# A two-layer hybrid model step on one core: feed-forward input as seven block products in place of eight, weight-block sums by adding transfers, output projection in six parts

## The chip, the cores and the metric

The kernel runs on one core of a Trainium2 chip. The metric is the device time of one execution in microseconds (us), lower is better. TensorE (PE) multiplies; VectorE (DVE), ScalarE (ACT) and GpSimd (POOL) work on vectors; SyncE (SP) issues most transfers. PSUM is the memory that matmuls write, in banks of 512 float32 for each of 128 partitions.

## What is computed

Two layers over 640 tokens (128 of context, 512 latent) of 1024 features. Each layer is a feed-forward half step, a token mixing and a second feed-forward half step, every one behind an RMS norm that is modulated by shift, scale and gate ("ada" rows, from a condition vector). The change is in the feed-forward:

```python
def swiglu(h, w_in, w_out):
    g, u = jnp.split(h @ w_in, 2, axis=-1)
    return (jax.nn.silu(g) * u) @ w_out

def layer(x, cond, p, lam_init, ropes, ctx):
    mods = (jax.nn.silu(cond) @ p['w_ada'] + p['b_ada']).reshape(cond.shape[0], N_MOD, 1, D_MODEL)
    ...
    h = modulate(rmsnorm(x, p['norm_ffn1']), sh1, sc1)
    x = x + 0.5 * g1 * swiglu(h, p['w_ffn1_in'], p['w_ffn1_out'])
    h = modulate(rmsnorm(x, p['norm_mix']), sh2, sc2)
    y, kv = token_mix(h, p, lam_init, ropes, ctx)
    x = x + g2 * y
    h = modulate(rmsnorm(x, p['norm_ffn2']), sh3, sc3)
    x = x + 0.5 * g3 * swiglu(h, p['w_ffn2_in'], p['w_ffn2_out'])
```

The feed-forward is 2816 wide, so `w_in` has 22 tiles of 128 columns for the gate and 22 for the value.

## The kernel before, in words

The residual stream is kept as 8 tiles `x[d]` of 128 features by 640 tokens. All large products are float32 in three passes: weight and activation are each split into a part `hi` that the multiplier takes exactly and a rest `lo`, and hi·hi, hi·lo and lo·hi are summed in PSUM. `split` (L166 to L168) makes an activation's two parts: ACT copies (L167), DVE subtracts (L168). `load_w` (L143 to L158) loads a weight block through SP into one of three `raw` buffers (L144), ACT makes `hi` (L156), DVE makes `lo` (L157).

The sublayers run in the order feed-forward (0,0), mix of layer 0, feed-forward (0,2), (1,0), mix of layer 1, (1,2), the last one with the final norm. A feed-forward (`ffn`) goes over 22 pairs of a gate tile and a value tile. `pair` takes for each of both a 512 KB weight block, and 8 contraction tiles x 3 passes x 2 halves of the tokens (320 and 322 columns; two columns carry the shift) are 48 matmuls into one PSUM tile `S` of two banks; there are two such tiles. DVE takes the product out of PSUM times the norm's factor `R` (L385), ACT applies silu (L421), DVE multiplies (L423), and `split` makes the pair's activation. After 8, 7 and 7 pairs (`PARTS`) the output projection `out` adds what these pairs give to all 8 tiles of `x` (`x_update`, L366). In the last part each `out` also prepares the next norm's tile (`Norm.tile`: squares on ACT L289, sum on POOL L291, scaled hi and lo L300 and L301).

Beside this runs the "pump": 131 steps that each load 512 KB of the ada weights and reduce them on DVE with two instructions (`dump`, L244). `tick` takes steps at a rate of 0.8, 0.8 and 0.55 in the first three feed-forwards: 2 x rate for a pair and 1 x rate for an `out`.

The order of the instructions on each engine is set when the program is built, by a scheduler of the framework: it takes the program in the order in which it is written, knows which tile each instruction reads and writes, and places semaphore waits between engines by whole tiles. Each engine then runs its own list in that order.

Of the kernel before, what the change touches and what calls it, by code (L numbers as in the profile page):

```python
# [20 lines left out]
NO, NE = 1, 6  # L21
# [15 lines left out]
PARTS = ((0, 8), (8, 15), (15, 22))  # L37
# [4 lines left out]
# the two halves of the tokens, without and with the columns of the shift  # L42
# [4 lines left out]
# columns of the per-partition vector table  # L47
# [28 lines left out]
def hybrid_step(ctx: ExitStack, tc: tile.TileContext, x_in, cc_in, cb_in, w_ada0, w_ada, pv_in, lam_in, w_fin, w_fout, w_min, w_mout,  # L76
# [7 lines left out]
    up = ctx.enter_context(tc.tile_pool(name="up", bufs=35))  # L84
    tp = ctx.enter_context(tc.tile_pool(name="tp", bufs=5))
    sp = ctx.enter_context(tc.tile_pool(name="sp", bufs=32))
# [17 lines left out]
    def E(dt=F32):  # L104
        return tp.tile([128, N], dt, tag="e", name=nm("e"), bufs=5)
# [37 lines left out]
    def load_raw(src, n):  # L143
        raw = wp.tile([128, 1024], F32, tag="raw", name=nm("raw"), bufs=3)  # L144
        nc.sync.dma_start(raw[:, :n], src)
        return raw

    def load_w(src, n, eng=None):
        """DRAM [128, n] -> (hi, lo) with hi + lo the weights exactly."""
        raw = load_raw(src, n)  # L150
        return split_w(raw, n, eng)

    def split_w(raw, n, eng=None):
        hi = wp.tile([128, 1024], F32R, tag="hi", name=nm("hi"), bufs=2)
# [17 lines left out]
    def lambdas():  # L172
        lv = T()
        nc.sync.dma_start(lv[:, :L * 128], lam_in)
        for l in range(L):
# [11 lines left out]
            lam.append(lm)  # holds -(lambda)  # L187
# [11 lines left out]
    def ada_direct(c, loads):  # L199
        """the products; yields before the row is turned into columns."""  # L200
# [20 lines left out]
    def silu_rows():  # L221
        """silu of the two conditions, along the free dimension of every partition."""
# [38 lines left out]
    def gate_tiles(l, sub):  # L261
        if sub == 1:
            return [mods[l][2 * (3 * sub + 2) + h] for h in range(2)]
        r = []
        for h in range(2):
            t = C([128, 4, 2], name="gate")
            V.tensor_scalar(out=t, in0=mods[l][2 * (3 * sub + 2) + h], scalar1=0.5, scalar2=None, op0=ALU.mult)
            r.append(t)
        return r

    class Norm:
        """Prepares the moving operand of the next sub-layer tile by tile."""
# [49 lines left out]
        def stats_spread(self):  # L322
# [4 lines left out]
            R = tp.tile([128, TX], F32, tag="R", name=nm("R"), bufs=1)  # L327
            G.memset(R[:, N:TX], 1.0)
            S.activation(R[:, :512], pa, AF.Copy)
            S.activation(R[:, 512:N], pb[:, :128], AF.Copy)  # L330
            self.R = R

# [10 lines left out]
    def mm3(ps, cuts, hi, lo, acts, ks=range(KT), start=True, stop=True, hs=(0, 1)):  # L343
        """ps[h] (+)= w^T act over contraction tiles, three passes."""
        for i, k in enumerate(ks):
            w0, w1 = hi[:, k * 128:(k + 1) * 128], lo[:, k * 128:(k + 1) * 128]
            ah, al = acts[k]
            for p, (w, a) in enumerate(((w0, ah), (w0, al), (w1, ah))):
                for h in hs:
                    c0, c1 = cuts[h]  # L350
                    mm(ps[h][:, :c1 - c0], w, a[:, c0:c1],
                       start and i == 0 and p == 0, stop and i == len(ks) - 1 and p == 2)

    def halves(p):
        """the two halves of the tokens with the shift, side by side across the banks of p."""
# [5 lines left out]
    def x_update(d, ps, gate):  # L361
        """x[d] += gate * ps, ps holding the two halves of the tokens."""
# [7 lines left out]
    def ffn(l, sub, norm, nxt, pump, prate):  # L370
# [11 lines left out]
        def pair(i):  # L382
            def evac(ps):
                t = T()
                V.tensor_tensor(out=t[:, :TX], in0=whole(ps), in1=norm.R, op=ALU.mult)  # L385
                return t
# [948 lines left out]
```

## Time and profile before

| what | value |
|---|---|
| time, median of 3 executions | 2506.04 us (2505.41 to 2507.21) |
| the profiled execution's span | 2509.4 us |
| PE busy | 2446.1 us, 97% |
| DVE busy | 1563.7 us, 62% |
| ACT busy | 865.5 us, 34% |
| POOL busy | 304.9 us, 12% |
| bytes moved by transfers | 282.10 MB |

Busy time is the union of an engine's instructions over the span of the profiled execution. A mean over the span hides that stages differ, so the rows further down are windows of single stages.

### The profile page before, as it was taken

Reading aid. Unit: us, or ns where it says so; the run is one execution under the profiler, and the core shown is the slowest. Engines: PE = TensorE matmul, PEld = TensorE weight load, DVE = VectorE, ACT = ScalarE, POOL = GpSimd, SP = SyncE. Lnnn points to the kernel's source line nnn. Section 1 sums busy time; section 2 is a strip of 40 time slices with the busy share of each in tenths; the row PEclk is TensorE's granted clock in tenths of the full one; section 3 lists DMA queues with packets and bytes.
Section 4 is the critical chain, followed back from the end, with each engine's and each line's share of the span. In section 5 each row is a group of like instructions: output and inputs, shape, how many; then the busy total and the mean of one; then the engine's idle time right before and its main releaser. Section 6 shows DMA issues by size and latency. Waiting matters only on the chain. (4 is left out here: it accounts for less than half of the span.)

```text
span 2509.4 us, 39961 instructions
## 1 busy us (share of the span) xinstructions
PE 2446.1 (97%) x16529; PEld 2405.3 (96%) x16529; DVE 1563.7 (62%) x2550; ACT 865.5 (34%) x1417; POOL 304.9 (12%) x329
## 2 busy tenths in 40 slices
PE   8999999998998999999999999999999999999998
PEld 4999999998898999999999999999989999999998
DVE  5766766668886666666666556556788664334335
ACT  3222212356664221212332122224666442122223
POOL 3000000143224000000110000003513230000002
PEclk8999999999999999999999999999999999999999
DMA  7444444224322444444333333332242122222224
GB/s 261 154 142 136 132 138 138 90 89 137 117 66 89 137 135 135 133 137 135 101 110 110 120 115 116 115 102 89 90 143 85 53 74 70 75 76 70 82 72 130
DMA packets 91317, 282.10 MB, mean 112 GB/s; under 512 B 9600, under 2 KB 17664, under 8 KB 91136
## 3 DMA queue, kind: packets, MB, share of 16 engines
q1 hardware_dynamic: 91136, 279.56, 34.6%
q8 instruction: 130, 2.13, 0.3%
q14 instruction: 51, 0.42, 0.1%
HBM read 264.58 MB, written 14.94 MB: 111 GB/s over the span
## 5 line engine op out<-in xcount | busy, mean ns | idle before, releaser
L128 PE MATMUL S<-u,hi 128*128 128x320 f32 (+1 forms) x9056 | 1720.7, 311 | 14.8 <-DVE x L366 7.3
L128 PEld LDWEIGHTS S<-u,hi 128*128 128x128 f32 x9056 | 1434.7, 189 | 18.8 <-ACT hi L156 7.7
L128 PE MATMUL S<-u,lo 128*128 128x320 f32 (+2 forms) x4528 | 1047.6, 310 | 4.4 <-DVE lo L157 4.4
L128 PEld LDWEIGHTS S<-u,lo 128*128 128x128 f32 x4528 | 765.2, 189 | 5.4 <-DVE lo L157 5.4
L156 ACT ACTIVATE hi<-raw 128x1024 fp32r<-128x1024 f32 (+2 forms) x336 | 345.2, 1027 | 1117.7 <-PE S L128 649.9
L244 DVE SCALAR_TENSOR_TENSOR dump<-raw,sc 128x1024 f32<-128x1024 f32 x262 | 322.9, 1234 | 175.9 <-DMA raw<-in_w_ada_dram 172.7
L157 DVE TENSOR_TENSOR lo<-raw,hi 128x1024 fp32r<-128x1024 f32 (+1 forms) x296 | 351.3, 1187 | 10.7 <-ACT hi L156 8.0
L385 DVE TENSOR_TENSOR t<-S,R 128x642 f32<-128x642 f32 x176 | 145.2, 825 | 331.8 <-PE S L128 325.2
L128 PE MATMUL F<-u,hi 128*128 128x320 f32 (+1 forms) x1056 | 236.9, 316 | 3.9 <-DVE t L547 3.3
L366 DVE SCALAR_TENSOR_TENSOR x<-S,gate,x 128x128 f32<-128x128 f32 (+2 forms) x264 | 99.8, 433 | 184.8 <-PE S L128 184.6
L128 PEld LDWEIGHTS F<-u,hi 128*128 128x128 f32 x1056 | 175.1, 190 | 5.5 <-DVE t L547 3.8
L128 PE MATMUL F<-u,lo 128*128 128x320 f32 (+1 forms) x528 | 155.2, 313 | 0.0
L167 ACT ACTIVATE u<-t 128x640 fp32r<-128x640 f32 x88 | 65.1, 740 | 208.4 <-DVE t L423 208.4
L157 POOL TENSOR_TENSOR lo<-raw,hi 128x1024 fp32r<-128x1024 f32 (+1 forms) x40 | 89.4, 2234 | 258.3 <-ACT hi L156 212.2
L168 DVE TENSOR_TENSOR u<-t,u 128x640 fp32r<-128x640 f32 x88 | 72.6, 825 | 62.1 <-ACT u L167 62.1
L421 ACT ACTIVATE t<-t 128x128 f32<-128x128 f32 (+1 forms) x176 | 89.6, 556 | 57.2 <-DVE t L385 55.1
L301 DVE SCALAR_TENSOR_TENSOR u<-x,scl,u 128x128 fp32r<-128x128 f32 x96 | 94.3, 996 | 7.9 <-ACT u L300 6.9
L128 PEld LDWEIGHTS F<-u,lo 128*128 128x128 f32 x528 | 97.6, 190 | 0.0
L291 POOL TENSOR_TENSOR t<-t,t 128x640 f32<-128x640 f32 x42 | 73.5, 1749 | 161.6 <-ACT t L289 161.4
L568 POOL MEMSET pl<- 128x8 f32 x4 | 0.4, 107 | 761.2 <-DVE dump L244 761.1
L423 DVE SCALAR_TENSOR_TENSOR t<-t,t 128x128 f32<-128x128 f32 (+1 forms) x176 | 88.7, 545 | 0.0
L716 DVE TENSOR_REDUCE s<-S 128x1 f32<-128x640 f32 x96 | 77.4, 814 | 2.7 <-PE S L128 2.4
(184 smaller groups left out, 1382.6 us busy)
## 6 DMA issues: line engine op xcount, KB each, us to landing
raw<-in_w_fin_dram SPq DMA_DIRECT2D x176, 512.0 KB
raw<-in_w_ada_dram SPq DMA_DIRECT2D x131, 512.0 KB
raw<-in_w_fout_dram SPq DMA_DIRECT2D x72, 448.0 KB
raw<-in_w_min_dram SPq DMA_DIRECT2D x36, 512.0 KB
raw<-in_w_fout_dram SPq DMA_DIRECT2D x32, 512.0 KB
u<-in_w_ada_dram SPq DMA_DIRECT2D x24, 256.0 KB
KS<-kd SPq DMA_DIRECT2D x16, 384.0 KB
raw<-in_w_mout_dram SPq DMA_DIRECT2D x16, 384.0 KB
```

The source lines that it names most:

```text
L128: PE.matmul(out, lhsT, rhs, start=start, stop=stop)
L156: S.activation(hi[:, :n], raw[:, :n], AF.Copy)
L157: (eng or V).tensor_tensor(out=lo[:, :n], in0=raw[:, :n], in1=hi[:, :n], op=ALU.subtract)
L168: V.tensor_tensor(out=dst_lo, in0=src, in1=dst_hi, op=ALU.subtract)
L244: V.scalar_tensor_tensor(out=dump[:, :D], in0=raw, scalar=1.0, in1=rows[i], op0=ALU.mult, op1=ALU.mult, accum_out=m[0][:, b, i:i + 1])
L291: G.tensor_tensor(out=sq[:, :N], in0=sq[:, :N], in1=self.acc[:, :N], op=ALU.add)
L301: (eng or V).scalar_tensor_tensor(out=lo[:, a:b], in0=x[d][:, a:b], scalar=s, in1=hi[:, a:b], op0=ALU.mult, op1=ALU.subtract)
L366: V.scalar_tensor_tensor(out=xs, in0=ps[h][:, a:b], scalar=g[:, d % 4, c:c + 1], in1=xs, op0=ALU.mult, op1=ALU.add)
L385: V.tensor_tensor(out=t[:, :TX], in0=whole(ps), in1=norm.R, op=ALU.mult)
L421: S.activation(g[:, a:b], g[:, a:b], AF.Silu, bias=g[:, N + c:N + c + 1])
L423: V.scalar_tensor_tensor(out=u[:, a:b], in0=u[:, a:b], scalar=u[:, N + c:N + c + 1], in1=g[:, a:b], op0=ALU.add, op1=ALU.mult)
L716: V.tensor_reduce(out=m, in_=s[:, :, :HN], axis=AX.XY, op=ALU.max, negate=True)
```

## The change

`FastNorm` takes the place of `Norm` ahead of the four feed-forwards: it holds the normed activation in four blocks (features 0 to 511 or 512 to 1023, first or second half of the tokens with its shift columns, 322 columns each) and stores seven matrices in hi and lo: three of the blocks and the four sums N1, T3, N2 and T4 (for feed-forward (0,0) the four blocks, and the sums after pair 0).

`pair` takes the gate and value weights as the other matrix of four blocks (`a11`, `a12` for the gate, `a22` and the rest for the value) and makes seven products of 4 contraction tiles x 3 passes = 12 matmuls of 322 columns, 84 in all, where there were 96. Weight sums are made by transfers: `take` loads 256 KB through SP, `add` issues a transfer on POOL's queue that adds 256 KB from DRAM into the buffer, `copy` is a copy on ACT; S2 = S1 copied + a21's block added, S4 = S2 copied + one more block. Products 1, 3, 5 and 7 go into bank A of the pair's tile `p`, 4 and 6 into bank D, 2 into a tile `B` of the pool `F`; where a sum is needed both before and after more products, ACT copies bank A or D to SBUF in between (L625, L633, L638) and DVE adds what comes later (L630, L643, L646, L649 to L651). The first two pairs of (0,0) are made in the old way (`plain_pair`). Weights are split in pieces of 512 columns with four `hi` and four `lo` buffers, and there are seven `F` buffers for the sums. The output projection runs in six parts of 4, 4, 4, 4, 3 and 3 pairs, its update of `x` in two instructions instead of three, in the order 0, 4, 1, 5, 2, 6, 3, 7.

```diff
-PARTS = ((0, 8), (8, 15), (15, 22))
+PARTS = ((0, 4), (4, 8), (8, 12), (12, 16), (16, 19), (19, 22))
+UB = 36
+RAWB = 3
+HLB = 4
+FB = 7
+NPLAIN = 2
+ORDER = (0, 4, 1, 5, 2, 6, 3, 7)
+HW = N // 2 + 2
...
+    class Weights:
...
+        def piece(src, eng=None):
+            n = src.shape[-1]
+            hi = wp.tile([128, 512], F32R, tag="hi", name=nm("hi"), bufs=HLB)
+            lo = wp.tile([128, 512], F32R, tag="lo", name=nm("lo"), bufs=HLB)
+            S.activation(hi[:, :n], src, AF.Copy)
+            (eng or V).tensor_tensor(out=lo[:, :n], in0=src, in1=hi[:, :n], op=ALU.subtract)
+            return hi, lo
...
+    class FastNorm:
...
+        def sums(self, k, b1, b2, late=False):
...
+            V.tensor_tensor(out=T3, in0=B22, in1=B12, op=ALU.subtract)
+            V.scalar_tensor_tensor(out=N2, in0=T3, scalar=-1.0, in1=B11, op0=ALU.mult, op1=ALU.subtract)
+            form("N2", N2)
+            form("T3", T3)
+            V.tensor_tensor(out=N1, in0=B11, in1=B12, op=ALU.subtract)
+            form("N1", N1)
+            V.scalar_tensor_tensor(out=T4, in0=N2, scalar=-1.0, in1=B21, op0=ALU.mult, op1=ALU.subtract)
+            form("T4", T4)
...
+    def product(ps, piece, act, start):
+
+        hi, lo = piece
+        for k in range(4):
             w0, w1 = hi[:, k * 128:(k + 1) * 128], lo[:, k * 128:(k + 1) * 128]
...
+            ah, al = act[k][:, 0], act[k][:, 1]
+            for p, (w_, a) in enumerate(((w0, ah), (w0, al), (w1, ah))):
+                PE.matmul(ps, w_, a, start=start and k == 0 and p == 0, stop=k == 3 and p == 2, skip_group_check=True)
...
+        def pair(i, first):
...
+            rg = load_raw(wi[i, 0], 1024)
+            a11, a12 = rg[:, :512], rg[:, 512:]
...
+            def take(src):
+                t = FT([128, 512])
+                nc.sync.dma_start(t, src)
+                return t
+
+            def add(t, src):
+                G.dma_start(t, src, accum_op=ALU.add)
+
+            def copy(src):
+                t = FT([128, 512])
+                S.activation(t, src, AF.Copy)
+                return t
...
+            s1, s3, a22 = take(wi[i, 1, :, :512]), take(wi[i, 0, :, :512]), take(wi[i, 1, :, 512:])
+            add(s1, wi[i, 1, :, 512:])
+            add(s3, wi[i, 1, :, :512])
+            s2 = copy(s1)
+            add(s2, wi[i, 0, :, :512])
+            piece = Weights.piece
+            p = PS()
+            A, D, B = p[:, 0, :HW], p[:, 1, :HW], PF()[:, :HW]
+            g, u = T(), T()
+            w = piece(a11)
+            product(A, w, norm.get("B11"), True)
+            S.activation(g[:, :HW], A, AF.Copy)
+            w = piece(a12)
+            product(B, w, norm.get("B21"), True)
+            if first:
+                norm.stats_sum()
+            V.tensor_tensor(out=g[:, :HW], in0=B, in1=g[:, :HW], op=ALU.add)
+            w = piece(s2)
+            product(A, w, norm.get("N2"), False)
+            S.activation(u[:, :HW], A, AF.Copy)
+            w = piece(s3)
+            s4 = copy(s2)
+            add(s4, wi[i, 0, :, 512:])
+            product(D, w, norm.get("T3"), True)
+            S.activation(u[:, HW:], D, AF.Copy)
+            if first:
+                norm.stats_spread()
+            w = piece(s1)
+            product(A, w, norm.get("N1"), False)
+            V.tensor_tensor(out=u[:, HW:], in0=A, in1=u[:, HW:], op=ALU.add)
+            w = piece(a22)
+            product(D, w, norm.get("T4"), False)
+            V.tensor_tensor(out=u[:, :HW], in0=D, in1=u[:, :HW], op=ALU.add)
+            w = piece(s4)
+            product(A, w, norm.get("B22"), False)
+            V.tensor_tensor(out=g[:, HW:], in0=A, in1=norm.R[:, HW:], op=ALU.mult)
+            V.tensor_tensor(out=g[:, :HW], in0=g[:, :HW], in1=norm.R[:, :HW], op=ALU.mult)
+            V.tensor_tensor(out=u, in0=u, in1=norm.R, op=ALU.mult)
+            activation(i, g, u, HN)
```

Three places show how the instructions now stand. In their names the number is the tile's; `waits` names the engines or transfer queues whose semaphores an instruction waits for (DMASW are the transfers on POOL's queue, DMAHW those on SP's).

PE in the last feed-forward, before: the end of one group of 48 matmuls and the start of the next (`u` is the activation, `hi` and `lo` the weight's parts).

```order
L128 MATMUL S_15492<-u_12549,hi_15488 128x322
L128 MATMUL S_15492<-u_12548,lo_15489 128x320
L128 MATMUL S_15492<-u_12548,lo_15489 128x322
L128 MATMUL S_15562<-u_12097,hi_15558 128x320 [waits DVE_49,Activation_49]
L128 MATMUL S_15562<-u_12097,hi_15558 128x322
```

PE in the last feed-forward, after the change: the end of product 3 (`hi_25158`) and the start of product 4 (`hi_25175`) of one pair.

```order
L498 MATMUL S_25120<-u_23195,hi_25158 128x322 x2
L498 MATMUL S_25120<-u_23195,lo_25159 128x322
L498 MATMUL S_25120<-u_22927,hi_25175 128x322 [waits Activation_49]
L498 MATMUL S_25120<-u_22927,hi_25175 128x322
L498 MATMUL S_25120<-u_22927,lo_25176 128x322 [waits DVE_49]
```

Further on in the same pair: the end of product 4, two matmuls of the next pair (`S_25269`) and the start of product 5 (`hi_25195`).

```order
L498 MATMUL S_25120<-u_23198,hi_25175 128x322 x2
L498 MATMUL S_25120<-u_23198,lo_25176 128x322
L498 MATMUL S_25269<-u_22916,hi_25273 128x322 [waits DVE_49,Activation_49]
L498 MATMUL S_25269<-u_22916,hi_25273 128x322
L498 MATMUL S_25120<-u_22931,hi_25195 128x322 [waits Activation_49]
L498 MATMUL S_25120<-u_22931,hi_25195 128x322
L498 MATMUL S_25120<-u_22931,lo_25196 128x322 [waits DVE_49]
```

Between the last matmul of one product and the first of the next there is now a wait for ACT, where before the next group had a tile of its own; the first matmul of product 4 waits for the copy of line 633 that reads the other bank, and that of product 5 for the copy of line 638.

ACT in the last feed-forward, before, one pair:

```order
L156 ACTIVATE hi_15813<-raw_15811 128x1024 [waits DMAHW6_49,PE_49,Activation_49]
L421 ACTIVATE t_15738<-t_15738 128x128 [waits DVE_49]
L421 ACTIVATE t_15738<-t_15738 128x512
L156 ACTIVATE hi_15870<-raw_15868 128x1024 [waits DMAHW7_49,PE_49,Activation_49]
L167 ACTIVATE u_15801<-t_15795 128x640 [waits DVE_49]
```

ACT after the change, the stretch of the same pair as on PE (`f` are the buffers of the weight sums; L610 is `copy`):

```order
L610 ACTIVATE f_25266<-f_25258 128x512 [waits DMASW0_49,DVE_49]
L543 ACTIVATE t_24973<-t_24973 128x514 [waits DVE_49]
L166 ACTIVATE hi_25212<-f_25113 128x512 [waits DMAHW1_49,PE_49]
L188 ACTIVATE u_25103<-t_24974 128x640 [waits DVE_49]
L166 ACTIVATE hi_25229<-f_25179 128x512 [waits DMASW7_49,PE_49]
L633 ACTIVATE t_25123<-S_25120 128x322 [waits PE_49]
L610 ACTIVATE f_25328<-f_25266 128x512 [waits DMASW2_49,Activation_49]
L543 ACTIVATE t_25122<-t_25122 128x128 [waits DVE_49]
L166 ACTIVATE hi_25273<-raw_25256 128x512 [waits DMAHW7_49,PE_49]
L638 ACTIVATE t_25123<-S_25120 128x322 [waits PE_49]
L166 ACTIVATE hi_25290<-raw_25256 128x512 [waits PE_49]
```

Each of the two copies out of PSUM stands behind a weight conversion that itself waits for PE, and the second `copy` (f_25328) stands between them and waits for a transfer of POOL's queue.

POOL after the change, where nothing stood in the feed-forward before: the last adding transfer of one pair and the four of the next.

```order
L606 DMA f_25179<-in_w_fin_dram 128x512 [waits DMASW0_49,DVE_49,Activation_49]
L606 DMA f_25258<-in_w_fin_dram 128x512 [waits DMAHW5_49,DMAHW2_49,DVE_49]
L606 DMA f_25260<-in_w_fin_dram 128x512 [waits DMAHW3_49,DMASW3_49,DVE_49]
L606 DMA f_25266<-in_w_fin_dram 128x512 [waits DMASW5_49,DMASW2_49,Activation_49]
L606 DMA f_25328<-in_w_fin_dram 128x512 [waits DMASW4_49,DVE_49,Activation_49]
```

Of the four, the first two wait for SP's load of the buffer, the last two for ACT's copy into it.

## Rows read from the trace of the kernel before

**Rows 1.** The page: span, busy time, and the TensorE clock in 40 slices (tenths).
```profile
span 2509.4 us, 39961 instructions
PE 2446.1 (97%) x16529; PEld 2405.3 (96%) x16529; DVE 1563.7 (62%) x2550; ACT 865.5 (34%) x1417; POOL 304.9 (12%) x329
PEclk8999999999999999999999999999999999999999
```
**Rows 2.** Windows: feed-forward (200, 900, 1400, 2100) and mixing (600, 1800), busy times, clock, DMA.
```profile
core 0: us, PE busy (x) PEld busy (x) DVE busy (x) ACT busy (x) POOL busy (x), PEclk, DMA share, GB/s
200.00:300.00 100.00, 100.00 (x681) 100.00 (x681) 63.95 (x97) 24.98 (x33) 0.00 (x0) 1.00 0.40 131
900.00:1000.00 100.00, 100.00 (x684) 100.00 (x683) 63.58 (x105) 21.36 (x26) 0.00 (x0) 1.00 0.44 134
1400.00:1500.00 100.00, 100.00 (x681) 100.00 (x680) 52.24 (x83) 21.16 (x25) 0.00 (x0) 1.00 0.38 120
600.00:700.00 100.00, 91.59 (x637) 88.17 (x636) 83.92 (x166) 64.57 (x146) 23.49 (x15) 0.98 0.37 126
1800.00:1900.00 100.00, 92.08 (x656) 88.31 (x655) 83.06 (x170) 67.58 (x154) 23.08 (x22) 1.00 0.39 135
2100.00:2200.00 100.00, 100.00 (x682) 100.00 (x681) 37.62 (x56) 21.55 (x25) 0.00 (x0) 1.00 0.24 74
```
**Rows 3.** Groups of PE by form: count, busy us, mean ns, idle before.
```profile
L128 PE MATMUL S<-u,hi 128*128 128x320 f32 x5824 | 1441.7, 311 | 11.6 <-DVE x L366 7.3 <-ACT hi L156 3.2 <-DVE u L301 0.9
```
**Rows 4.** Groups of ACT by form, the same columns.
```profile
L156 ACT ACTIVATE hi<-raw 128x1024 fp32r<-128x1024 f32 x248 | 263.0, 1060 | 858.9 <-PE S L128 491.3 <-issue 350.0 <-PE F L128 7.6
L167 ACT ACTIVATE u<-t 128x640 fp32r<-128x640 f32 x88 | 65.1, 740 | 208.4 <-DVE t L423 208.4
L421 ACT ACTIVATE t<-t 128x512 f32<-128x512 f32 x88 | 62.4, 709 | 0.0
L167 ACT ACTIVATE p<-S 128x512 fp32r<-128x512 f32 x64 | 38.2, 597 | 26.9 <-DVE p L168 17.0 <-PE H L128 4.8 <-PE S L731 4.2
L167 ACT ACTIVATE p<-H 128x256 fp32r<-128x256 f32 x36 | 13.7, 380 | 0.1
L156 ACT ACTIVATE hi<-raw 128x768 fp32r<-128x768 f32 x16 | 13.5, 841 | 6.1 <-PE F L128 2.8 <-issue 2.3 <-ACT u L300 1.0
```
**Rows 5.** Timeline near the end: start us, duration us, engine, line, operation.
```profile
2480.86 0.54 PE L476 MATMUL H<-ident,s 128*128 128x128 f32 x3 [0.49 <-POOL s L340]
...
2481.44 0.49 ACT L478 ACTIVATE R<-H 128x384 f32<-128x384 f32 x1 [3.14 <-PE H L476]
...
2481.83 0.95 ACT L156 ACTIVATE hi<-raw 128x896 fp32r<-128x896 f32 x1
```
**Rows 6.** Groups of DVE by form, columns as in rows 3.
```profile
L244 DVE SCALAR_TENSOR_TENSOR dump<-raw,sc 128x1024 f32<-128x1024 f32 x262 | 322.9, 1234 | 175.9 <-DMA raw<-in_w_ada_dram 172.7
...
L168 DVE TENSOR_TENSOR u<-t,u 128x640 fp32r<-128x640 f32 x88 | 72.6, 825 | 62.1 <-ACT u L167 62.1
L423 DVE SCALAR_TENSOR_TENSOR t<-t,t 128x512 f32<-128x512 f32 x88 | 65.6, 745 | 0.0
...
L423 DVE SCALAR_TENSOR_TENSOR t<-t,t 128x128 f32<-128x128 f32 x88 | 30.4, 345 | 0.0
...
L547 DVE TENSOR_TENSOR t<-F,R 128x322 f32<-128x322 f32 x24 | 11.7, 488 | 9.4 <-PE F L128 9.3
...
L666 DVE TENSOR_TENSOR t<-t,t 128x512 f32<-128x512 f32 x10 | 6.9, 687 | 0.2
L665 DVE TENSOR_TENSOR t<-t,u 128x512 f32<-128x512 f32 x10 | 6.8, 680 | 0.0
```
**Rows 7.** Timeline: a 512 KB load issued by SP, and the DVE instruction that waited for it.
```profile
1006.35 0.33 SPq L145 DMA_DIRECT2D raw<-in_w_ada_dram  x1
...
1009.86 1.23 DVE L244 SCALAR_TENSOR_TENSOR dump<-raw,sc 128x1024 f32<-128x1024 f32 x1 [0.97 <-DMA raw<-in_w_ada_dram]
```
**Rows 8.** The page: transfer queues (packets, MB, share of 16 engines) and the largest issue.
```profile
q1 hardware_dynamic: 91136, 279.56, 34.6%
...
raw<-in_w_fin_dram SPq DMA_DIRECT2D x176, 512.0 KB
```

More of the change, by code (lines that the diff above doesn't have):

```diff
@@ L384, in evac, with plain_pair, half @@
+        def plain_pair(i):
+            def half(ps, w, h):
+                n = (HN, HW)[h]
+                for k in range(KT):
+                    w0, w1 = w.at(k)
+                    a = norm.f[norm.blocks(k)[h], k % 4]
+                    ah, al = a[:, 0, :n], a[:, 1, :n]
+                    for p, (w_, a_) in enumerate(((w0, ah), (w0, al), (w1, ah))):
+                        mm(ps[:, :n], w_, a_, k == 0 and p == 0, k == KT - 1 and p == 2)
+            def evac(p, sign):
                 t = T()
-                V.tensor_tensor(out=t[:, :TX], in0=whole(ps), in1=norm.R, op=ALU.mult)
@@ L495, in ffn @@
             for i in range(k0, k1):
-                pair(i)
+                if l == 0 and sub == 0 and i < NPLAIN:
+                    plain_pair(i)
+                    if i == 0:
+                        for k in range(4):
+                            norm.late(k)
+                else:
+                    pair(i, i == 0)
+            while gate is None and mods[l][2 * (3 * sub + 2) + 1] is None:
+                pump.step()
             gate = gate or gate_tiles(l, sub)
@@ L501, in ffn @@
             else:
-                for d in range(KT):
+                for d in ORDER:
                     out(k0, k1, d, gate, nx)
@@ L797, in mix @@
         rq8 = [None, None]
-        kxs = [sp.tile([128, 2, 128], F32R, tag="kc", name=nm("kx"), bufs=3) for _ in range(2)]
+        kxs = [FT([128, 2, 128], F32R, "kx") for _ in range(2)]
         gvcx = vctx_tiles()
@@ L1044, in mix_sum @@
         def mix_sum(w, ps, d, start, stop):
-            hi, lo = w
-            mm3(ps, CN, hi, lo, y, range(6), start, stop)
+            mm3(ps, CN, w, y, range(6), start, stop)
         def mix_ends():
@@ L1139, in mix @@
         ends = mix_ends()
-        for d in range(KT):
+        for i, d in enumerate(ORDER):
             if d in opened:
@@ L1215, in hybrid_step @@
     ada_all(1, (2, 3, 0, 1, 4, 5, 8, 9, 6, 7))
-    nx = ffn(0, 2, nx, lambda: (pump.step(8), Norm(1, 0))[1], pump, RATES[1])
+    nx = ffn(0, 2, nx, lambda: (pump.step(8), FastNorm(1, 0))[1], pump, RATES[1])
     pump.step(1000)
```

256 lines of the change are left out of this document (174 added, 82 removed).

## The prediction

> **What bounds the kernel now.** I read the page first: one profiled execution spans 2509.4 us and TensorE (PE) is busy 2446.1 us of it, 97%, at a granted clock near full speed in every slice but the first [rows 1]. Three readings from the sequences of instructions matter next. The windows [rows 2] show what a stretch of feed-forward holds: PE busy 100.00 of 100 us with 681 to 684 matmuls, so one matmul costs 100/682 = 0.1466 us, while VectorE (DVE) is busy 38 to 64 us and ScalarE (ACT) 21 to 25 us. PE alone is the bound there. In the mixing stretches PE stands for 8 us of 100 and DVE is at 83%. A matmul's own record is 311 ns long [rows 3]: matmuls overlap, and a result is there 0.31 - 0.147 = 0.16 us after the next one could have started. That is nothing while the next matmul goes elsewhere, and it is the start of every wait below. By groups of one form I then took the durations of ACT [rows 4] and DVE [rows 6], by the timeline the overlap of two ACT instructions [rows 5], and the time of a load [rows 7].
>
> **What the change removes.** 86 of the 88 gate/up pairs go from 96 matmuls to 84 (the first two pairs stay as they are): 1,032 x 0.1466 = **-151 us**, if PE goes on without a gap. A pair's own PE time falls from 14.07 to 12.31 us. The output projection keeps its matmuls.
>
> **What it puts on ACT.** Per pair ACT had two conversions of 1024, two silu and one conversion of 640. Now it has seven conversions of 512, two copies of 512, three evacuations of 322 from PSUM, and the silu and conversion as before. A 512 conversion: from 1060 ns at 1024 and 841 at 768 [rows 4] it falls 0.855 ns an element, so 0.62 us. A 322 evacuation lies between 380 ns (256) and 597 (512): 0.44. The next ACT instruction starts about 0.10 before the last one's end (a 0.49 us one at 2481.44, the next at 2481.83 [rows 5]), so 0.52 and 0.34 each, one behind the other: 9 x 0.52 + 3 x 0.34 + about 1.6 = 7.3 us of 12.31. ACT is no bound by its sum; its place in the chain is what counts.
>
> **The waits between the seven products.** This is the term that decides. Products 3, 5 and 7 write bank A, 4 and 6 write bank D of one PSUM tile, and in the order of the change each waits for the reader of the other bank, because the tile is guarded as a whole. Before, each matmul group had a tile of its own and an earlier group's reader had 48 matmuls of time.
> - *Third to fourth product.* Nothing is queued on PE between them. ACT has a conversion (the last weight sum) ahead of the evacuation, and that conversion waits for the buffer which the last but one matmul of product 3 frees. With t the start of the last matmul: the buffer is free at t + 0.16, plus a hop. Hops are about 0.05 (PE's short group starts at 2480.86 and takes 0.54, ACT starts at 2481.44 [rows 5]). So 0.21 + 0.52 + 0.44 + 0.03 = t + 1.20 against t + 0.147: 1.05 us of standing. Bounds: 0.9, if a conversion in a row takes 0.44 (no fixed part) and the evacuation 0.37, and 1.3 with full durations. 86 x 1.05 = **+90 us** (77 to 112).
> - *Fourth to fifth.* The same chain with another conversion (the next pair's first block), but two matmuls of the next pair stand between: 1.05 - 2 x 0.147 = 0.76. 86 x 0.76 = **+65 us** (52 to 86).
> - *Fifth to sixth, sixth to seventh.* Five matmuls of the next pair (0.73 us) stand between, and the reader is DVE: 0.16 + 0.05 + 0.49 (322 from PSUM [rows 6]) = 0.70. Hidden: 0, up to 0.2 us each where DVE comes late (0 to 34 us).
>
> So feed-forward pairs take 12.31 + 1.05 + 0.76 = 14.12 us against 14.07: the removed matmuls come back as gaps.
>
> **Adding transfers.** 344 transfers on POOL's queue, four a pair, add a 256 KB block into a buffer; POOL is free there (no POOL instruction in the feed-forward windows [rows 2]). The chain is: copy, add, copy, add. ACT's second copy waits for the first copy's add, and the conversion that frees the fifth product stands behind it. From the end of the first copy to the latest harmless start of the second I count: seventh product's tail, products 2 and 3 of the next pair, a gap of 1.05 and the slack behind it, about 4.1 us. No add is in the trace. From below: a 512 KB load took 1009.86 - 1006.35 = 3.51 us from issue to its reader [rows 7]; half the bytes gives less. From above: the same 3.5 us plus 2 us for a second reading and for POOL's part, 5.5. I take 3.5, nearest to the only row, so 0; the upper end is 86 x 1.4 = +120 us. By the Trainium skill, page "DMA: Bandwidth & Descriptors", section "Anatomy of one DMA — SWDGE (gpsimd) path", such a transfer takes 2.0 us plus its bytes over 436 GB/s, an estimate of 2.6 us; by it the term is 0 too, with more room; no run here shows one.
>
> **DVE and the pump.** Per pair DVE has seven 512 subtractions (0.60 in a row, from 680 to 687 ns), five of 322 (0.40), one of 644 (0.75), two silu products (0.9), one 640 subtraction (0.75): 4.2 + 2.0 + 0.75 + 0.9 + 0.75 = 8.6 us, some 6 before. The pump adds two dumps of 1234 ns a step, 1.6 steps a pair at rate 0.8: 4.0. So 12.6 of 14.1 us. DVE's order then just meets PE's; it also waited 172.7 us on 131 pump loads, 1.3 each [rows 6]. With six parts there are 48 outputs an FFN instead of 24, each half as long (24 x 0.1466 = 3.52 us), each still with 0.8 step: 1.0 + 0.6 + 2.0 = 3.6 us of DVE. I take 0.3 us a pair for the 35 pairs or so that pump and 0.2 us for their 70 outputs: 10 + 14 = **+25 us** (0, if the gaps of PE cover it, to 110, if each pump load is waited for).
>
> **Parts and transitions.** 24 parts instead of 12, each end with a chain from the last product to the first output that needs it: DVE 0.49, silu 0.71, product 0.75, conversion 0.74, hops: 3.0 us, against about 20 matmuls queued in between (2.9): 0.3 each, **+7 us** (0 to 25). The last part has 3 tiles instead of 7, so its eight outputs take 21 us of PE instead of 49, and the next norm must fit beside it. The new norm costs DVE 11 instructions of 322 for each two tiles (44 x 0.45 = 20), with the updates (8 x 1.0) and weights (8 x 0.5) 32 us; so some 10 us stick out at the second feed-forward of the first layer, and I put 5 on each of the three other places where a norm is made (two mixes before, two behind, less at the start): **+25 us** (0 to 50). Loads: 258 of 256 KB and 90 of 512 KB for 176 of 512 KB, and the adds; 282 MB become some 395, so the queues' 34.6% of the engines' time [rows 8] about 48%: 0.
>
> **Sum.** -151 + 90 + 65 + 0 + 25 + 7 + 25 = +61: span 2509.4 becomes 2570. The median of the runs before, 2506.0, is 3.4 below that span, so **2567 us**; from here on the numbers are for the median. This kernel's measurement tells 0.2% (5 us) from no change.
>
> **Rivals.**
> - *The waits are shorter, or hidden: faster.* If the two waits are 0.75 and 0.45 us (conversion done before the product ends, so only the evacuation counts), they give 103 us back; with nothing lost in parts, norm or pump: -48, 2458; with half of those 57 us lost, 2486. It decides from a sum of both waits below (151 - 57)/86 = 1.1 us with my other terms, or below 1.76 without them. For it: PE was 100% busy wherever it had work, and the other engines had a third of their time free. Against: both waits are in the order, and the rows give 1.8.
> - *Exactly given back.* With the other terms covered and the waits at 1.76: 2501 to 2511.
> - *The adds land late.* Above 4.1 us each further 0.1 us costs 8.6 us; 5.0 us gives 2567 + 77 = 2644. For it: a transfer that must read its destination as well. Against: half the bytes of the load at 3.5.
> - *DVE becomes the bound while the pump runs*, through its loads (three buffers, shared with the weights): 2567 + 85 = 2652.
> - *The clock falls because PE stands twice a pair.* In the mixing windows PE stood 8 us of 100 and the granted clock was 0.98 and 1.00, so at the 2.4 GHz level [rows 2]; 2% of some 2,000 us would add 40: 2607. The Trainium skill, page "TensorE: Matmul & The Clock Gate", section "A second HAM failure mode: psum-queue depth-cycling", tells of a kernel whose PE stood briefly between groups and whose clock went to and fro between the levels; the mixing rows do not show it.
> - *The change does not do what it says*: the order has 16,414 and 15,384 matmuls, so it does.
>
> **Chances.** Forecast 0.45 (own range 2530 to 2610); shorter waits 0.28; given back 0.08; adds 0.11; DVE 0.05; clock 0.03. So slower 0.64, same 0.08, faster 0.28. The range reaches into the faster case down to 2465 (waits at about 0.85 and 0.5 us with the rest covered) and up to 2660, which takes in the late adds at 5.2 us and the pump.
>
> **What would show it.** Right: matmuls 15,4xx; in feed-forward windows about 590 to 600 matmuls per 100 us (84 in 14.1), PE at 86 to 88%, PE's idle time put down to ACT's evacuations (the two 322 copies of line 633 and 638) at near 1 us each; clock at 1.00. Wrong: 650 or more matmuls per 100 us (waits hidden); PE's idle put down to DVE in the first two feed-forwards only (pump); ACT's copy waiting on a transfer of POOL's queue (adds); a lower granted clock.

## The result, and the profile after the change

The changed kernel takes 2850.36 us (median of 4, 2839.52 to 2854.63); the kernel before, run beside it, 2506.62 (2505.41 to 2507.79). The ratio is 1.1365 [1.1342, 1.1387]: 343.7 us slower, where 61 were forecast. The sign was right; the size was off by 283 us, and 2850 lies far outside the range that ended at 2660. The profiled execution spans 2837.8 us.

The page of the changed kernel, the same parts as [rows 1, 8]; the last row is an issue of transfers: count, KB each, median us from issue to landing.

```profile
span 2837.8 us, 42654 instructions
...
PE 2465.9 (87%) x15497; PEld 2320.2 (82%) x15497; DVE 1961.5 (69%) x3666; ACT 1296.1 (46%) x2587; POOL 610.2 (22%) x717
...
PEclk8899999999998999999989999999999999999998
...
q1 hardware_dynamic: 129728, 300.02, 31.9%
q0 software_dynamic: 49536, 90.20, 19.8%
...
f<-in_w_fin_dram POOLq DMA_DIRECT2D x344, 256.0 KB, 5.3
```

PE has 1,032 matmuls fewer, as announced (15,497 for 16,529; the prediction's 15,384 and 16,414 stand in neither trace), and is yet busy 20 us longer: busy time counts a matmul at half clock in full, and also the end of the last matmul before every standing. It also stands for 372 us of the span (2837.8 - 2465.9), where it stood for 63. Where, the windows show (columns as in [rows 2]; feed-forward at 200, 900, 1400 and 2500, mixing at 600).

```profile
200.00:300.00 100.00, 86.12 (x543) 81.56 (x542) 78.72 (x147) 38.06 (x70) 14.75 (x17) 0.98 0.68 184
900.00:1000.00 100.00, 81.00 (x474) 76.33 (x473) 80.87 (x148) 45.03 (x92) 22.71 (x22) 0.90 0.61 159
1400.00:1500.00 100.00, 79.75 (x465) 74.51 (x464) 73.31 (x140) 56.44 (x122) 30.28 (x31) 0.90 0.50 123
600.00:700.00 100.00, 95.02 (x660) 90.44 (x660) 73.93 (x149) 65.02 (x145) 39.56 (x46) 1.00 0.34 102
2500.00:2600.00 100.00, 92.31 (x595) 87.93 (x594) 55.16 (x97) 43.24 (x79) 16.56 (x19) 1.00 0.54 127
```

The last feed-forward, the only one without the pump, does 595 matmuls in 100 us, inside the 590 to 600 that the prediction named. That is luck: the prediction counted pairs alone (84 in 14.1 us), but a window holds the outputs too. Four pairs of 14.12 us and eight outputs of 3.52 us are 528 matmuls in 84.6 us, so its own working gives 624 in 100 us; 595 come about because a pair takes 14.8 us and eight outputs with the end of their part 29.2. PE is busy 92% in this window, not 86 to 88%. The three with the pump do 465 to 543, and two of these windows have a mean granted clock of 0.90.

One pair of that last feed-forward, from its timeline (start us, duration us, engine, line, operation; in brackets the idle time before and what ended it):

```profile
2506.25 0.31 PE L498 MATMUL S<-u,lo 128*128 128x322 f32 x1
2506.78 0.42 ACT L633 ACTIVATE t<-S 128x322 f32<-128x322 f32 x1
2507.10 0.62 ACT L166 ACTIVATE hi<-f 128x512 fp32r<-128x512 f32 x1
2507.26 0.57 PE L498 MATMUL S<-u,hi 128*128 128x322 f32 x2 [0.70 <-ACT t L633]
...
2508.94 0.63 ACT L610 ACTIVATE f<-f 128x512 f32<-128x512 f32 x1 [1.22 <-DMA f<-in_w_fin_dram]
2508.99 0.31 PE L498 MATMUL S<-u,lo 128*128 128x322 f32 x1
2509.48 0.61 ACT L166 ACTIVATE hi<-raw 128x512 fp32r<-128x512 f32 x1
...
2510.00 0.42 ACT L638 ACTIVATE t<-S 128x322 f32<-128x322 f32 x1
2510.15 0.89 PE L498 MATMUL S<-u,hi 128*128 128x322 f32 x4 [0.84 <-ACT hi L166]
```

Product 3's last matmul starts at 2506.25, product 4's first at 2507.26: 1.01 us, of which 0.15 are the matmul's own. The median over this feed-forward is 1.06 us of standing here and 0.73 ahead of the next pair's first product, against 1.05 and 0.76 forecast. To what PE's waits in the products are put down in the whole trace (us in all, times, longest):

```profile
PE S L498 <- ACT t L633: 92.5, 85, 4.8
PE S L498 <- ACT hi L166: 49.5, 59, 3.3
```

and that conversion in e2 below, which has no adds, in the last feed-forward (timeline):

```profile
2417.28 0.63 ACT L166 ACTIVATE hi<-raw 128x512 fp32r<-128x512 f32 x1 [1.99 <-PE S L498]
2417.81 0.42 ACT L638 ACTIVATE t<-S 128x322 f32<-128x322 f32 x1
```

The first standing is the one forecast. The second is put down to the weight conversion of line 166 and not to the evacuation of line 638 (4 times, 6.9 us): PE's next two matmuls are the next pair's, their conversion waits for product 4 (there are four `hi` buffers), and the evacuation behind it ends in time for product 5. In e5 below, where bank D has a tile of its own, product 5 follows product 4 at once and both standings are gone.

A row "x2" lasts 0.57 behind a wait and 0.46 elsewhere: the second matmul after a standing comes 0.25 us after the first, not 0.15. That happens four times a pair.

With the pump the same places look like this (timeline of the changed kernel in feed-forward (1,0)):

```profile
2339.10 0.31 PE L498 MATMUL S<-u,lo 128*128 128x322 f32 x1
2341.05 0.63 ACT L610 ACTIVATE f<-f 128x512 f32<-128x512 f32 x1 [4.67 <-DMA f<-in_w_fin_dram]
2341.58 0.71 ACT L543 ACTIVATE t<-t 128x514 f32<-128x514 f32 x1
...
2343.76 0.42 ACT L633 ACTIVATE t<-S 128x322 f32<-128x322 f32 x1
...
2344.23 0.65 PE L498 MATMUL S<-u,hi 128*128 128x322 f32 x2 [4.82 <-ACT t L633]
2344.68 0.47 PE L498 MATMUL S<-u,lo 128*128 128x322 f32 x1
```

Read backwards: PE stands 4.82 us and the view names ACT's evacuation of line 633. But product 3, which that evacuation reads, ended at 2339.4 (2339.10 + 0.31). From then on it stood in ACT's queue behind the copy of line 610, and this had waited 4.67 us for an adding transfer, that of S1; from the copy's start at 2341.05 ACT then needed 2.7 us to come to the evacuation. The releaser named is the last link; the wait began two links earlier. The windows of this stretch show what comes after:

```profile
2336.00:2339.70 3.70, 3.41 (x24) 3.15 (x22) 1.64 (x4) 0.38 (x1) 0.09 (x1) 1.00 0.87 171
2339.70:2344.50 4.80, 0.27 (x2) 0.27 (x3) 2.18 (x4) 3.15 (x6) 0.86 (x1) 1.00 0.53 92
2344.60:2348.00 3.40, 2.96 (x12) 2.56 (x10) 0.83 (x3) 1.69 (x5) 1.01 (x2) 0.50 0.67 189
2348.00:2352.00 4.00, 3.98 (x25) 3.78 (x26) 1.82 (x3) 0.92 (x2) 1.61 (x2) 1.00 0.87 132
```

24 matmuls in 3.7 us at 2.4 GHz, then the standing, then 3.4 us at 0.50, the 1.2 GHz level, with 12 matmuls, then 2.4 GHz again. So this standing is paid for twice. In the whole trace 32 such stretches add up to 208.5 us (6 with 35.1 us before); with half of PE's busy time in them taken as lost, they cost 77 us, against 11 before.

### The profile page after: what moved, and what is told of

Read it like the earlier page. It is cut to its first block, busy times and chain, and to the rows that moved or that the text cites. A ratio compares the mean times of both kernels' runs of the same rounds, so it can differ in the third digit from the quotient of the medians.

```text
span 2837.8 us, 42654 instructions
## 1 busy us (share of the span) xinstructions
PE 2465.9 (87%) x15497; PEld 2320.2 (82%) x15497; DVE 1961.5 (69%) x3666; ACT 1296.1 (46%) x2587; POOL 610.2 (22%) x717
## 3 DMA queue, kind: packets, MB, share of 16 engines
q0 software_dynamic: 49536, 90.20, 19.8%
## 5 line engine op out<-in xcount | busy, mean ns | idle before, releaser
L498 PE MATMUL S<-u,hi 128*128 128x322 f32 x4128 | 975.7, 325 | 184.4 <-ACT t L633 92.5
L135 PE MATMUL S<-u,hi 128*128 128x320 f32 (+3 forms) x3552 | 716.2, 319 | 89.9 <-DVE x L523 22.7
L606 POOL DMA_DIRECT2D f<-in_w_fin_dram x344 | 299.9, 931 | 1656.5 <-ACT f L610 903.4
L498 PE MATMUL S<-u,lo 128*128 128x322 f32 x2064 | 637.7, 314 | 0.3 <-DVE lo L167 0.3
L166 ACT ACTIVATE hi<-raw 128x512 fp32r<-128x512 f32 (+1 forms) x492 | 296.6, 606 | 683.2 <-PE S L498 286.1
L166 ACT ACTIVATE hi<-f 128x512 fp32r<-128x512 f32 x430 | 270.6, 630 | 368.0 <-PE S L498 250.8
L135 PE MATMUL S<-u,lo 128*128 128x320 f32 (+3 forms) x1776 | 423.5, 315 | 2.6 <-DVE lo L167 2.6
L167 DVE TENSOR_TENSOR lo<-raw,hi 128x512 fp32r<-128x512 f32 (+1 forms) x412 | 278.2, 680 | 133.4 <-ACT hi L166 127.3
L167 DVE TENSOR_TENSOR lo<-f,hi 128x512 fp32r<-128x512 f32 x430 | 293.3, 685 | 32.5 <-ACT hi L166 28.2
L523 DVE SCALAR_TENSOR_TENSOR x<-S,gate,x 128x128 f32<-128x128 f32 x368 | 183.6, 544 | 135.2 <-PE S L135 134.7
L135 PEld LDWEIGHTS F<-u,hi 128*128 128x128 f32 x1056 | 180.7, 195 | 12.5 <-DVE t L779 6.9
L610 ACT ACTIVATE f<-f 128x512 f32<-128x512 f32 x172 | 107.6, 625 | 109.0 <-DMA f<-in_w_fin_dram 102.8
```

What stands on the lines that cost most here:

```text
L135: PE.matmul(out, lhsT, rhs, start=start, stop=stop)
L166: S.activation(hi[:, :n], src, AF.Copy)
L167: (eng or V).tensor_tensor(out=lo[:, :n], in0=src, in1=hi[:, :n], op=ALU.subtract)
L498: PE.matmul(ps, w_, a, start=start and k == 0 and p == 0, stop=k == 3 and p == 2, skip_group_check=True)
L523: V.scalar_tensor_tensor(out=x[d][:, a:b], in0=w[:, a:b], scalar=g[:, d % 4, c:c + 1], in1=x[d][:, a:b], op0=ALU.mult, op1=ALU.add)
L606: G.dma_start(t, src, accum_op=ALU.add)
```

## The experiments

Three theories stood at the start. **Guard**: the waits between products, because banks A and D belong to one tile. **Adds**: the adding transfers come late and ACT's queue stands behind them. **Everything else**: DVE and pump, six parts, or buffers that the change took from other stages. Runs e1 to e4 had kernels before of 2506.75 us beside them, e5 to e8 2507.78, e9 to e12 2505.17. e1 was run four times (2769.69 to 2783.47 us), every other kernel of this section once.

**Guard and adds, each taken away.** e1_split gives product bank D a tile of its own:

```diff
-            A, D, B = p[:, 0, :HW], p[:, 1, :HW], PF()[:, :HW]
+            A, B, D = p[:, 0, :HW], PF()[:, :HW], PF()[:, :HW]
```

> The changed kernel with bank D of a pair in a PSUM tile of its own, so that products 4 and 6 no longer wait for the readers of bank A, nor 5 and 7 for those of bank D. Theory 'whole-tile guard' (the two waits of 1.06 and 0.73 us a pair, with the slow second matmul behind each, cost most of the loss in the pairs): pairs without pump fall from 14.8 to 12.6-13.2 us, the whole to 2600-2690 us. Rival 'late adds' (the adding transfers, 5.3 us from issue to landing, set the pace of a pair): pairs stay above 14 us, the whole above 2760 us.

e2_noadd keeps the tile and leaves the adding transfers out:

```diff
-                G.dma_start(t, src, accum_op=ALU.add)
+                pass
```

> The changed kernel without its 344 adding transfers: the weight blocks are loaded and copied, but not added (the sums S1 to S4 are left out, so the output is not the reference's). Theory 'whole-tile guard': pairs without pump stay at 14.6-14.8 us; only what the pump's feed-forwards lose more comes down, the whole to 2770-2820 us. Rival 'late adds': pairs fall to below 13.5 us everywhere and the whole to 2690 us or less.

e5_split_noadd has both edits:

> Both at once: bank D in a tile of its own and the 344 adding transfers left out (the sums of the weight blocks are not formed, so the output is not the reference's). Theory 'guard and adds together hold the pair up, one behind the other': without either a pair takes 12.6-13.3 us, and the whole 2600-2670 us. Rival 'a third thing holds the pair' (ACT's conversions with only four buffers): pairs stay at 14 us or more, the whole above 2700 us.

e6_split_plain has the tile of its own, and plain transfers of the same size on the same queue in place of the adding ones (`G.dma_start(t, src)`):

> As e1_split, with the 344 transfers of POOL's queue plain instead of adding (they overwrite the block; the sums are left out). Same queue, same bytes from DRAM. Theory 'the adding makes them slow': landing falls from 5.3 to 3-3.5 us, pairs to 12.6-13.5 us, the whole to 2620-2690 us. Rival 'POOL's queue itself is slow': landing stays at 4.5 us or more and the whole above 2740 us.

Measured: e1 2775.39 us, ratio to before 1.1081 [1.1057, 1.1104]; e2 2745.6; e5 2525.85; e6 2590.72. e1 came out in its rival's range and e2 between its two, so neither theory alone is the loss; e5 and e6 came out faster than either of their ranges. By stages, in us from the first to the last pair's instruction of line 651 on DVE (outputs and, in the middle one, the way between two feed-forwards included):

| kernel | (0,0), 20 pairs | (0,2) and (1,0), 44 pairs | (1,2), 22 pairs, no pump | time |
|---|---|---|---|---|
| neither (e5) | 390.5 | 863.0 | 399.6 | 2525.85 |
| guard alone (e2) | 424.6 | 979.0 | 451.4 | 2745.6 |
| adds alone (e1) | 432.5 | 986.8 | 458.0 | 2775.39 |
| both (the change) | 447.9 | 1033.4 | 457.0 | 2850.36 |
| plain transfers alone (e6) | 393.0 | 903.9 | 406.9 | 2590.72 |

Either alone costs 220 or 250 us; both together 325, not 470. So what each is worth depends on the order in which they go: taken out of the change as it stands, the guard is worth 75 us (the change less e1) and the adds 105 (the change less e2). In the last feed-forward it is simply the larger of the two: 451.4 and 458.0 alone, 457.0 together. Taking away one of them shows almost nothing there, because the other one sets the pace. Without both, PE has no gap away from the pump (e5, windows):

```profile
200.00:300.00 100.00, 94.46 (x632) 93.08 (x631) 94.10 (x177) 40.90 (x75) 0.00 (x0) 1.00 0.56 172
2200.00:2300.00 100.00, 100.00 (x673) 99.42 (x673) 60.72 (x107) 41.15 (x75) 0.00 (x0) 1.00 0.31 95
```

673 matmuls in 100 us at 2200; at 200, beside the pump, DVE is at 94% and PE at 632. How the adds alone can set a pace, ACT's timeline of e1 in the last feed-forward shows:

```profile
2561.39 0.63 ACT L610 ACTIVATE f<-f 128x512 f32<-128x512 f32 x1 [3.87 <-DMA f<-in_w_fin_dram]
2561.93 0.42 ACT L633 ACTIVATE t<-S 128x322 f32<-128x322 f32 x1
...
2570.12 0.63 ACT L610 ACTIVATE f<-f 128x512 f32<-128x512 f32 x1 [0.58 <-DMA f<-in_w_fin_dram]
...
2575.80 0.63 ACT L610 ACTIVATE f<-f 128x512 f32<-128x512 f32 x1 [3.06 <-DMA f<-in_w_fin_dram]
2576.34 0.42 ACT L633 ACTIVATE t<-S 128x322 f32<-128x322 f32 x1
```

and POOL's in the same stretch:

```profile
2562.32 1.76 POOL L606 DMA_DIRECT2D f<-in_w_fin_dram  x2 [5.40 <-ACT f L610]
2569.81 0.86 POOL L606 DMA_DIRECT2D f<-in_w_fin_dram  x1 [5.73 <-DVE lo L167]
2571.05 0.86 POOL L606 DMA_DIRECT2D f<-in_w_fin_dram  x1 [0.37 <-ACT f L610]
```

It is a ring. In e1's order each copy stands directly ahead of an evacuation, S4's ahead of line 633, S2's ahead of line 625. The copy for S4 (2561.39) lets POOL issue S4's add; the next pair's S1 add is behind it in POOL's queue (issued at 2562.98); it lands just before 2570.1, where the copy for S2 can start; S2's add is issued at 2571.05 and has landed at 2575.80, where the next S4 copy starts. This turn is 14.41 us with two landings in series (7.1 and 4.7 us), longer than the pair's own 12.5; where no outputs stand between, the turns of this feed-forward take 13.8 to 16.3 us, median 14.7. Each late landing is handed on to PE through the evacuation behind it. The guard's cycle is 14.8 us a pair (e2), the ring's 14.7; in the last feed-forward one covers the other. With the pump both get longer and no longer coincide.

What a landing costs, page of e6 (plain) and then, in a second fence, of the change (adding): the issue with its median landing, and POOL's own time for it.

```profile
L606 POOL DMA_DIRECT2D f<-in_w_fin_dram x344 | 185.6, 540 | 1509.1 <-ACT f L610 1100.5
...
f<-in_w_fin_dram POOLq DMA_DIRECT2D x344, 256.0 KB, 3.8
```

```profile
L606 POOL DMA_DIRECT2D f<-in_w_fin_dram x344 | 299.9, 931 | 1656.5 <-ACT f L610 903.4
```

Adding lands after 5.3 us in place of 3.8 and takes 0.93 us of POOL in place of 0.54. In time: plain transfers cost 65 us (e6 less e5), that they add 185 more (e1 less e6).

**Attention's buffers.** The change also lets the exponentials' tiles of the attention come out of the activations' pool, and halves the pool of small tiles. This part of the diff stands outside the core that was shown; e8_mem makes it alone in the kernel before, e9_sp16 only its last line:

```diff
-    up = ctx.enter_context(tc.tile_pool(name="up", bufs=35))
+    up = ctx.enter_context(tc.tile_pool(name="up", bufs=36))
...
-        return tp.tile([128, N], dt, tag="e", name=nm("e"), bufs=5)
+        return up.tile([128, UW], dt, tag="U", name=nm("e"))
...
-    sp = ctx.enter_context(tc.tile_pool(name="sp", bufs=32))
+    sp = ctx.enter_context(tc.tile_pool(name="sp", bufs=16))
```

> The kernel before with the buffers of the attention as the change has them: the exponentials' tiles taken from the pool of the activations (36 buffers for both instead of 35 and 5), 16 small tiles instead of 32. Nothing else of the change. Theory 'fewer buffers slow the attention': the stretch from the first to the last exponential of a layer, 180 us before and 204-206 us in the changed kernel, takes 200 us or more here too, the whole 2545-2560 us. Rival 'the weights in pieces of 512 do it': the stretch stays at 180 us, the whole at 2505-2515 us.

> The kernel before with 16 small tiles instead of 32, nothing else: half of e8_mem's edit. Theory 'the small tiles (row maxima, factors, sums) run out': the attention's stretch is 200 us or more and the whole 2550-2565 us, as with both edits. Rival 'the exponentials' buffers do it': the stretch stays at 180 us, the whole at 2505-2512 us.

Measured: e8 2562.76 us, e9 2505.8. The small tiles cost nothing, the shared pool 57 us (e8 less e9; e8 less the kernel before beside it is 55). The stretch from the first to the last exponential, 180 and 178 us in the two layers before, takes 205 and 203 in e8, as in the changed kernel (206 and 203), and 179 and 178 in e9. Windows of the mixing stretch and PE's waits, e9 first, then e8:

```profile
600.00:700.00 100.00, 91.42 (x643) 87.74 (x642) 84.23 (x167) 65.09 (x146) 24.99 (x17) 1.00 0.36 122
1800.00:1900.00 100.00, 92.11 (x653) 88.30 (x652) 84.85 (x171) 68.08 (x153) 21.56 (x21) 1.00 0.38 136
```

```profile
600.00:700.00 100.00, 87.20 (x586) 83.08 (x585) 72.87 (x154) 60.75 (x138) 24.06 (x25) 0.93 0.36 121
1800.00:1900.00 100.00, 84.23 (x564) 79.29 (x563) 73.64 (x138) 59.41 (x128) 33.24 (x36) 0.94 0.30 105
...
PE H L128 <- DMA u<-qd: 17.8, 4, 8.5
```

643 and 653 matmuls become 586 and 564, and PE waits 17.8 us in all, up to 8.5 at once, for the loads of the queries (`u<-qd`), into a buffer of the pool from which the exponentials now draw; e9 has no such wait. The changed kernel has it too (12.0 us in all, one of 9.4).

**Six parts.** e4_parts gives the kernel before the six parts, and takes pump steps until the gates that a part needs are there:

```diff
-PARTS = ((0, 8), (8, 15), (15, 22))
+PARTS = ((0, 4), (4, 8), (8, 12), (12, 16), (16, 19), (19, 22))
...
+            while gate is None and mods[l][2 * (3 * sub + 2) + 1] is None:
+                pump.step()
```

> The kernel before with its output projection in six parts of 4, 4, 4, 4, 3 and 3 pairs, nothing else of the change. Theory 'parts are cheap': up to 1 us for each of 12 more part ends and some for the norms that stand behind a last part of 3 pairs, 2510-2540 us. Rival 'the parts themselves cost what the outputs lost' (118 us in the changed kernel): 2590-2630 us.

Measured: 2564.62, 58 us slower. Away from the pump a part's eight outputs take 28.4 us, close to their 28.15 of matmuls. Where the loss lies, the times of line 385 on DVE (it takes each product out of PSUM) tell, with 28.15 us of outputs that now come before the last pair and not behind it: of the 53 us by which the spans differ, 24 are inside the feed-forwards (10, 8 and 4 with the pump, 3 without) and 30 behind their last parts (5 to 10 each). Both are more than the theory had; the time lies between the two ranges.

**The pump.** e3_nodump is the change with the pump's DVE instructions over 64 columns instead of 1024; e10_rates is the change with lower rates.

> The changed kernel with the pump's DVE instructions over 64 columns instead of 1024 (15/16 of the reduction of the ada rows is left out); the pump's loads stay. Theory 'DVE is the bound while the pump runs': pairs and parts of the first three feed-forwards fall to those of the last (14.8 and 44 us), the whole by 90-130 us to 2710-2750 us. Rival 'late adds': the pump's feed-forwards stay slower than the last one, since its loads still share the transfer engines; the whole above 2790 us.

```diff
-RATES = (0.8, 0.8, 0.55)
+RATES = (0.6, 0.6, 0.41)
```

> The changed kernel with the pump at 0.6, 0.6 and 0.41 instead of 0.8, 0.8 and 0.55, so that a feed-forward with 48 outputs takes as many steps as one with 24 did. Theory 'the pump is too dense beside six parts': the first three feed-forwards lose 15-40 us less, 2810-2835 us. Rival 'the adds set those pairs too': within 10 us of 2850, since the number of steps in all is the same and fewer loads a pair only spread it.

Measured: e3 2809.92, e10 2863.86. DVE's part of the pump is worth 40 us of the 344, less than its theory had, and spreading it thinner gains nothing; the changed kernel's own four runs lie within 15 us.

**Can it be mended?** e7_split_sums keeps the tile of its own and lets POOL make the four sums from the two 512 KB blocks; e11_sums_rates adds the lower rates, e12_sums_sp32 to that the larger pool of small tiles.

```diff
-            add(s1, wi[i, 1, :, 512:])
-            add(s3, wi[i, 1, :, :512])
-            s2 = copy(s1)
-            add(s2, wi[i, 0, :, :512])
+            s1 = add(a21, a22, G)
+            s2 = add(s1, a11, G)
+            s3 = add(a11, a21, G)
+            s4 = add(s2, a12, G)
```

> As e1_split, but the four sums of a pair are made by POOL from the two 512 KB blocks that are in SBUF anyway (four raw buffers, five for the sums); no adding transfers, no copies on ACT, transfers back to those of the kernel before. Theory 'late adds': a sum takes POOL 1.3 us instead of 6 us from issue to landing, so pairs fall to 12.6-13.5 us and the whole to 2590-2680 us. Rival 'four sums of 1.3 us one behind the other, in front of buffers that are held longer, are as late': pairs at 14 us or more, the whole above 2720 us.

> As e7_split_sums (bank D apart, sums by POOL), with the pump at 0.6, 0.6 and 0.41. Theory 'DVE is the bound of those feed-forwards once the waits are gone': pairs of 14-18 us come down to 13-14.5, the whole by 30-60 us to 2630-2660 us. Rival 'POOL and DVE slow each other, pump or not': within 15 us of 2692.

> As e11_sums_rates, with 32 small tiles again and four buffers for the sums instead of five. Theory 'the small tiles run out': the attention's stretches go back to about 180 us, the whole 45-55 us below e11_sums_rates. Rival 'the exponentials' buffers do it', or four buffers for the sums hold the pairs up: no gain, or slower than e11_sums_rates.

Measured: e7 2692.43, e11 2672.28, e12 2672.9: the lower rates, which gained nothing in e10, give 20 us here (one run each), and the small tiles nothing again; e7 and e11 each lie between their two ranges. POOL's sums beat the transfers by 83 us (e7 against e1) and need 1.5 to 1.65 us each (by form, e7):

```profile
L605 POOL TENSOR_TENSOR f<-f,raw 128x512 f32<-128x512 f32 x172 | 278.8, 1621 | 120.4 <-issue 64.7 <-DVE lo L167 34.9 <-ACT t L626 12.0
```

In the last feed-forward this comes near e5 (654 to 663 matmuls in 100 us); beside the pump, in the window at 200, DVE is busy 97 us and PE does 536. None of the versions beats the kernel before, not even e5, which leaves the sums out. Giving e5 the attention's own buffers back would bring it to about 2469 (2525.85 - 57), an estimate that was not tried; and the sums, which cost 146 us in e11 (e11 less e5, at the lower rates), would still have to be made.

## Why the prediction was wrong, point by point

In differences between runs, a step at a time (runs of the changed kernel and of e1 scatter by up to 15 us, and most terms rest on one run; that e4's and e8's costs hold inside the changed kernel is assumed; guard and adds stand in the order of e2, and the other way round the adds have 250 and the guard 75):

| term | forecast | measured |
|---|---|---|
| removed matmuls | -151 | -151 (1,032 fewer; not timed alone) |
| guard: the two waits and what hangs on them | +155 | +220 (e2 less e5) |
| adds, beside the guard | 0, at most +120 | +105 (the change less e2) |
| attention's buffers | none | +57 (e8 less e9) |
| six parts and the norms behind them | +32 | +58 (e4 less before) |
| DVE, pump, all else | +25 | +54 (what is left of e5's +18) |

- **The two waits had the right size**: 1.06 and 0.73 us of standing, the second put down to the conversion and not, as announced, to the evacuation of line 638. What the term lacked is that PE does not go on at full pace: 0.10 us more at the second matmul after each of four standings, 0.42 a pair, and 0.149 us for a matmul where 0.1466 was read [rows 2] (100/673 in e5, 0.2 us a pair). So a pair takes 14.8 us, not 14.12. (1.06 + 0.73 + 0.07 + 0.42) x 86 = 196 of the guard's 220. The forecast of 590 to 600 matmuls was met in the last feed-forward by luck: two errors, the outputs left out of the count and the pair 0.7 us too short, cancel.
- **The step that failed first is "I take 3.5 ... so 0" for the adding transfers.** The price was taken from a plain load of SP [rows 7] with nothing for the addition; it is 5.3 us, near the upper end of 5.5. Worse, the limit of 4.1 us looked at one add between two copies. The order of POOL, which stood ahead of the prediction, has S4's add of one pair ahead of S1's of the next, so there are two landings in a pair's ring, and the ring (14.7 us a turn) is what has to be compared with the pair. The rival "the adds land late" named the mechanism and its sign, with 0.11 and 2644 us: too little of both. By the Trainium skill, page "DMA: Bandwidth & Descriptors", section "Anatomy of one DMA — SWDGE (gpsimd) path", the estimate was 2.6 us; e6 has 3.8 for plain transfers of that queue and the change 5.3 for adding ones, both beside the loads of SP's queue, so the measurement decides against it here.
- **The sum added terms that hide or raise each other.** Guard and adds stand on one queue of ACT. Where both are regular the longer hides the other; beside the pump, as the traces read, they shift against one another, with standings as long as the 4.82 us shown (no run shows the shifting by itself). The prediction asked of each term what covers it, but not what happens to the cover.
- **The clock**, a rival at 0.03, did fall: 77 us of PE time against 11, spread over the terms above, where that rival had 40 more. But it was not the two waits a pair that brought it down: the last feed-forward, with its standings of 1 us twice a pair, kept 1.00 (window at 2500). Nor is most of it due to guard and adds: e5, which has neither, still loses 55 us in 22 stretches (granted clock 0.971 over the run, 0.964 in the change). The prediction quoted the Trainium skill, page "TensorE: Matmul & The Clock Gate", on a clock that short pauses between groups bring down; the same page's section "HAM oscillation — how this bites in real kernels" tells of waits for transfers that do, and the stretch shown from feed-forward (1,0) agrees with that one: 0.50 behind 4.82 us of standing.
- **Attention's buffers were not priced at all.** The sum followed the engines and the feed-forward; a buffer pool that a stage elsewhere loses was in the diff as one line. It is a sixth of the loss.
- **Parts and transitions**: 32 against 58. Behind the last parts 30 came for 25 forecast; inside the feed-forwards 24 for 7, 21 of them beside the pump, where the prediction had put 14 for the outputs into its DVE term. The kernel in e4 has the old norm; what the new norm's entries cost was not measured alone.
- **DVE and pump**: 25 against 54 for all that is left. The trace of e5 (94% DVE at 200) speaks for DVE beside the pump, the 0.2 us a pair above is 17 of it, and the lower clock of e5, less what e4 and e8 lose by theirs, may be some 24 (an estimate from the half-clock stretches of the four traces); the rest was not split by a run.

Of what was to show it wrong, two signs came: ACT's copy waiting on POOL's transfers (102.8 us in the change, 248.5 in e1) and a lower granted clock. Of what was to show it right, the standings at line 633 came, near 1 us each (92.5 us in 85); those at line 638 did not.

## What to carry to other kernels

A producer chain that goes round through several queues (copy on ACT, issue on POOL, landing, copy) is a ring: add up one full turn, with each landing in it, and compare it with the period of the work that it feeds. When two waits sit on one in-order queue, remove both before judging either, since the longer hides the other. Read a diff's buffer lines as carefully as its instructions, and ask for each pool which other stage draws from it.

## What the hardware showed that was not expected

- An adding transfer of 256 KB: 5.3 us from issue to landing (4.0 for the fastest twentieth, 7 to 8 for the slowest) and 0.93 us on POOL; the plain one on the same queue 3.8 and 0.54. The 344 adding ones made 49,536 packets of the same 90.2 MB for which the plain ones made 27,520.
- The second matmul after a standing starts 0.25 us after the first, not 0.15, also after a standing of 0.07 us (product 6).
- Of the 32 stretches at half clock, 1.2 GHz, in the change, 27 came behind a standing of 1.8 to 9.4 us and five behind none longer than 1.3 us. More than ten standings of 1.9 to 3.4 us had none behind them. In the last feed-forward, with standings of 1 us twice a pair, the clock kept 1.00 from 2348 to 2798 us.
- e1, with no guard, has more half-clock time than the change (290.9 us in 54 stretches, against 208.5 in 32) and is still faster: PE stands 315 us in place of 372, in fewer standings of over 0.2 us (208 against 317) but more of over 1 us (119 against 92).
